# Down projection of nine pairs of feature tiles by seven block products in two passes

## The chip, the core and the metric

The kernel runs on one core of a Trainium2 chip. The core has a matrix engine (TensorE, PE in the profile, with its weight loads as PEld), a vector engine (VectorE, DVE), a scalar engine (ScalarE, ACT), a general engine (GpSimd, POOL) and a queue that issues transfers (SyncE, SP). The metric is the device time of one execution in microseconds; smaller is better.

## The reference

The reference is one decoder layer for 512 tokens of width 1024: a mixer sub-layer (two groups of attention heads), and behind it a SwiGLU channel mixer. Only the end of the channel mixer is touched here:

```python
h = rms_norm(x, ffn_pre_norm)
f = (silu(h @ w_gate) * (h @ w_up)) @ w_down      # 512 x 2816 times 2816 x 1024
x = x + rms_norm(f, ffn_post_norm)
```

D_FF is 2816, which makes 22 feature tiles of 128. All arithmetic is float32.

## The kernel before

**Float32 by three products.** PE multiplies operands of the type fp32r. Each float32 operand is split in two: a high part (ScalarE copies it into an fp32r tile) and a low part (VectorE subtracts the high part from the original). A product of two matrices is then three products in PSUM: high by high, low by high, high by low.

**The gate and up projections.** For feature tiles 3 to 21, `ff_prep` loads the weights of a tile, VectorE and ScalarE form and split block sums, and `ff_seven` multiplies by seven block products instead of eight (a scheme of Winograd's kind) into PSUM tiles called `gw`. VectorE and ScalarE carry the results out (`cy`, `cx`), apply the SiLU and write the feature tile `ffr[f]`: 128 features by 512 tokens, in float32.

**The down projection.** It is what the change replaces. The eight PSUM banks hold the whole output, four token tiles by two column halves (`acc[i][c]`, 128 by 512 each). For each of the 22 feature tiles `down_operands` loads 128 by 1024 weights (tile `wraw`, three buffers), splits them (`whi`, `wlo`) and splits the features (`ffh`, `ffl`); `down` then issues three matmuls of 128x512 for each of the eight banks, so 24 matmuls for a feature tile and 528 in all. For the first 19 feature tiles the loop runs over tiles; the last three (LAST = 3) run with the token tiles outside, so that token tile 0 is finished first and its norm and its output can start while PE works on the next.

**The end.** For each token tile ScalarE squares the two banks and sums them (`junk`), VectorE multiplies by the gain (`uf`), the root is taken in a few small instructions, VectorE scales and adds the residual, and the row goes out.

**What sets the order.** Nothing but the program's own order, and a list scheduler that places the instructions of each engine by its own estimate of times; each engine then executes its queue in that order, waiting on semaphores. `tc.issue_after(before[0])` ties a block product behind the one before it on PE. Tiles come from pools with a fixed number of buffers (`sslot`: 36 slots of 128x512; `big`: eight tiles of 128x1024 and two under the tag `ru`; weights: three each of `raw`, `hi`, `lo`), and an instruction that writes a buffer waits until the last reader of its former contents is done.

In the profile of before, the block products of the gate and up projections are L912, the matmuls of the down projection L1039, the split of weights L104 (ScalarE) and L114 (VectorE), the low part of the features L1033, the square sums L783, the gain L1058, the last scaling L1060, and the output L1061. GpSimd works in the attention part (L517, L672, L651) and in the norms in front of the channel mixer (L807, L819), and on nothing after that.

Of the kernel before, what the change touches and what calls it, by code (L numbers as in the profile page):

```python
# [80 lines left out]
def hybrid_block_kernel(  # L81
# [29 lines left out]
    def split_w(raw, w=1024, lo_eng=None, hi_eng="a"):  # L111
        hi, lo = split_slots()
        to_r(hi_eng, hi[:, :w], raw[:, :w])
        (lo_eng or dve).tensor_tensor(lo[:, :w], raw[:, :w], f32(hi[:, :w]), OP.subtract)  # L114
        return hi, lo
# [912 lines left out]

    def down_operands(f):
        w = split_w(load_w(wd[f]))  # L1030
        hi, lo = sslot("ffh"), sslot("ffl")
        to_r("a", hi, ffr[f])
        dve.tensor_tensor(lo, ffr[f], f32(hi), OP.subtract)  # L1033
        return w, hi, lo

    def down(i, ops, first, last, c):
        w, hi, lo = ops
        for n, (a, wi) in enumerate(((hi, 0), (lo, 0), (hi, 1))):
            pe.matmul(acc[i][c], a[:, i * P:(i + 1) * P],  # L1039
                      w[wi][:, c * SEQ:(c + 1) * SEQ],  # L1040
                      start=(first and n == 0), stop=(last and n == 2))
# [9 lines left out]
    ws = [down_operands(f) for f in range(NF - LAST, NF)]  # L1051
    for i in range(NT):
        for c in range(2):
            for n, ops in enumerate(ws):
# [3 lines left out]
        r = row_rsqrt(a, "c", lambda c: dve.tensor_tensor(uh[c], a[c], g_ffn[:, CS[c]], OP.mult))  # L1058
# [94 lines left out]
```

## Time and profile before

| | us |
|---|---|
| median of three runs | 698.28 (696.29 to 698.91) |
| the profiled execution, device time | 697.03 |
| its span, first to last instruction | 695.3 |
| PE busy in it | 662.0 (95%) |
| DVE busy | 507.7 (73%) |
| ACT busy | 365.3 (53%) |
| POOL busy | 79.0 (11%) |

The device time is 1.73 us more than the span; that part lies around the first and the last instruction. In the views, a row of the timeline or of a group gives start, duration, engine, source line, operation and tiles. Matmuls are pipelined: one of 128x512 is shown with 0.39 us, while the next one starts earlier than that. The column PEclk of the view by windows is the clock that was granted to PE, as a share of the full one.

### The profile page before, as it was taken

What the parts mean: (1) busy time and instruction counts of PE and PEld (TensorE: products, weight loads), DVE (VectorE), ACT (ScalarE), POOL (GpSimd) and SP (SyncE); (2) the same over time, 40 slices, a digit from 0 to 9 for tenths busy, and PEclk for the clock granted to TensorE, in tenths of its full rate; (3) what the DMA queues carried; (4) which work ended last, traced back from release to release, by engine and by line L of the source; (5) the groups of instructions that cost most, each with busy time, mean ns of one, the idle gap of its engine ahead of it and who ended that gap; (6) DMA issues with size and microseconds to landing.
All of it is one profiled execution on the core that took longest, in us unless ns stands there. A gap on an engine that the chain in (4) does not pass through costs nothing.

```text
span 695.3 us, 11168 instructions
## 1 busy us (share of the span) xinstructions
PE 662.0 (95%) x4237; PEld 585.9 (84%) x4237; DVE 507.7 (73%) x918; ACT 365.3 (53%) x775; POOL 79.0 (11%) x86
## 2 busy tenths in 40 slices
PE   8998999999999989998789999999999999999995
PEld 4986878899778877876788999999999998888884
DVE  3867877886999997478898888888888567322227
ACT  6444442556778976435664556555655466211213
POOL 0000000020744632205300000000000000000000
PEclk9999999999999999899899999999999999999998
DMA  8447678571142130165204332333232443233203
GB/s 299 152 137 241 206 256 317 173 255 68 30 130 69 32 107 1 60 203 221 91 32 130 114 121 92 113 102 122 91 111 103 138 135 91 91 99 113 92 1 122
DMA packets 27142, 87.94 MB, mean 126 GB/s; under 512 B 3536, under 2 KB 4432, under 8 KB 26192
## 3 DMA queue, kind: packets, MB, share of 16 engines
q1 hardware_dynamic: 27088, 87.23, 37.4%
q8 instruction: 33, 0.54, 0.3%
q14 instruction: 21, 0.17, 0.1%
HBM read 75.16 MB, written 12.06 MB: 125 GB/s over the span
## 4 chain that ended last, share of the span: by engine, by line
PE 77%; DVE 12%; ACT 4%; DMA 3%; issue 2%; SPq 0%; DVEq 0%; ACTq 0%
PE gw L912 27%; PE acc L1039 17%; PE fm L289 8%; PE gu L892 4%; PE dv L363 3%; PE mixp L683 2%; PE tr L508 2%; DMA wraw<-in_wf 2%; PE avn L636 2%; PE vg L385 2%; PE sc L492 2%; DVE nm L496 2%; PE mix L695 2%; PE sc L493 1%; PE av L559 1%
## 5 line engine op out<-in xcount | busy, mean ns | idle before, releaser
L114 DVE TENSOR_TENSOR wlo<-wraw,whi 128x1024 fp32r<-128x1024 f32 (+2 forms) x58 | 69.9, 1208 | 83.7 <-ACT whi L104 81.1
L104 ACT ACTIVATE whi<-wraw 128x1024 fp32r<-128x1024 f32 (+2 forms) x58 | 60.5, 1046 | 108.5 <-PE acc L1039 66.6
L1039 PE MATMUL acc<-whi,ffl 128*128 128x512 f32 x176 | 68.5, 389 | 0.0
L1039 PE MATMUL acc<-wlo,ffh 128*128 128x512 f32 x176 | 68.0, 389 | 0.0
L1039 PE MATMUL acc<-whi,ffh 128*128 128x512 f32 x176 | 67.1, 390 | 0.4 <-ACT ffh L104 0.4
L517 POOL TENSOR_TENSOR p<-p,l 128x384 f32<-128x384 f32 (+3 forms) x60 | 49.9, 859 | 145.0 <-DVE l L547 88.6
L498 ACT ACTIVATE p<-sc,nm 128x128 f32<-128x128 f32 (+1 forms) x96 | 50.2, 530 | 19.9 <-DVE nm L496 19.5
L496 DVE TENSOR_REDUCE nm<-sc 128x1 f32<-128x128 f32 (+1 forms) x96 | 42.5, 482 | 10.5 <-PE sc L494 7.3
L512 ACT ACTIVATE pth<-tr 128x384 fp32r<-128x384 f32 (+1 forms) x60 | 31.5, 527 | 17.8 <-PE tr L508 17.6
L1039 PEld LDWEIGHTS acc<-whi,ffh 128*128 128x128 f32 x176 | 33.0, 188 | 7.4 <-ACT ffh L104 0.6
L1039 PEld LDWEIGHTS acc<-wlo,ffh 128*128 128x128 f32 x176 | 33.0, 188 | 6.9
L1039 PEld LDWEIGHTS acc<-whi,ffl 128*128 128x128 f32 x176 | 33.0, 188 | 6.8
L289 PE MATMUL fm<-xh,whi 128*128 128x512 f32 x128 | 33.9, 402 | 4.8 <-ACT whi L104 4.8
L513 DVE TENSOR_TENSOR ptl<-tr,pth 128x384 fp32r<-128x384 f32 (+1 forms) x60 | 34.9, 592 | 2.7 <-ACT pth L512 2.5
L492 PE MATMUL sc<-kst,qst 128*128 128x128 f32 (+2 forms) x96 | 35.4, 369 | 1.5 <-DVE pc L593 1.2
L508 PE MATMUL tr<-ident,p 128*128 128x128 f32 x200 | 33.5, 279 | 1.1 <-ACT pct L610 0.7
L289 PE MATMUL fm<-xh,wlo 128*128 128x512 f32 x128 | 33.4, 393 | 0.0
L289 PEld LDWEIGHTS fm<-xh,whi 128*128 128x128 f32 x128 | 23.8, 190 | 11.0 <-ACT whi L104 5.9
L289 PE MATMUL fm<-xl,whi 128*128 128x512 f32 x128 | 32.8, 392 | 0.0
L493 PE MATMUL sc<-kst,qst 128*128 128x128 f32 (+2 forms) x96 | 31.0, 323 | 0.0
L289 PEld LDWEIGHTS fm<-xl,whi 128*128 128x128 f32 x128 | 23.9, 188 | 5.0
L289 PEld LDWEIGHTS fm<-xh,wlo 128*128 128x128 f32 x128 | 23.7, 188 | 4.7
(292 smaller groups left out, 1749.7 us busy)
## 6 DMA issues: line engine op xcount, KB each, us to landing
wraw<-in_wg SPq DMA_DIRECT2D x22, 512.0 KB, 3.4
wraw<-in_wd SPq DMA_DIRECT2D x22, 512.0 KB, 3.4
wu<-in_wu SPq DMA_DIRECT2D x19, 512.0 KB, 3.4
wraw<-in_wf SPq DMA_DIRECT2D x16, 512.0 KB, 4.7
qk<-rope SPq DMA_DIRECT2D x7, 1024.0 KB, 4.8
kst<-qk SPq DMA_DIRECT2D x24, 256.0 KB, 4.2
qst<-qk SPq DMA_DIRECT2D x16, 256.0 KB, 2.8
wraw<-in_wo SPq DMA_DIRECT2D x8, 512.0 KB, 4.3
```

Source lines behind the costliest of these rows:

```text
L104: act.activation(dst, src, AF.Copy)
L114: (lo_eng or dve).tensor_tensor(lo[:, :w], raw[:, :w], f32(hi[:, :w]), OP.subtract)
L289: pe.matmul(pt, w[:, k * P:(k + 1) * P], xx[k], start=(n == 0), stop=(n == 3 * NK - 1))
L492: pe.matmul(sv, lhs, kk[:, 0, :w], start=True, stop=False)
L493: pe.matmul(sv, lhs, kk[:, 1, :w], start=False, stop=False)
L496: dve.tensor_reduce(nm, sv, AX.X, OP.max, negate=True)
L498: act.activation(pt, sv, AF.Exp, bias=nm, accum_out=l[:, i:i + 1])
L508: pe.transpose(tr[:, n * P:(n + 1) * P], pts[i][:, j * P:(j + 1) * P], ident)
L513: dve.tensor_tensor(ptl[:, sl], trv, f32(pth[:, sl]), OP.subtract)
L517: pool.tensor_tensor(p, p, l.to_broadcast(list(p.shape)), OP.mult)
L912: m = pe.matmul(pt, ww[:, k * P:(k + 1) * P], hx[k], start=(start and n == 0), stop=(n == 11), skip_group_check=True)
L1039: pe.matmul(acc[i][c], a[:, i * P:(i + 1) * P], w[wi][:, c * SEQ:(c + 1) * SEQ], start=(first and n == 0), stop=(last and n == 2))
```

## The change

The first 18 feature tiles are taken as nine pairs (PAIRS = 9). For a pair p the product is 512 tokens x 256 features times 256 features x 1024 columns. Each side is cut into 2 x 2 blocks: the tokens into halves (TL, TH), the features into the two tiles (a0, a1), the columns into halves (L, H). The product then takes seven products of blocks, with sums of blocks as operands, instead of eight. A block product is 256 tokens x 128 features x 512 columns, which is 2 token tiles x 3 matmuls = 6 matmuls of 128x512 (`down_mul`). It is done in two passes over the nine pairs, since the partial results don't fit in PSUM at once:

- the x pass: three block products a pair (18 matmuls) into `ca`, `cb`, `cc`. `x_load` fetches 1.5 weight tiles and VectorE subtracts two halves; `x_split` has GpSimd add two quarter blocks of the features (`s1`), and ScalarE and VectorE split weights (`whi`, `wlo`), three quarter blocks of features (`ah`, `al`) and the third weight block (`b21h`, `b21l`).
- the y pass: four block products a pair (24 matmuls) into `cd`, `ca`, `cb`, `cc`. `y_load` fetches the pair's two weight tiles again, and GpSimd subtracts two halves; `y_split` has GpSimd form three sums of feature blocks in place, VectorE two sums of weight blocks, and the two engines split two weight tiles (the second into the tiles `hth`, `htl`, which are free by then) and two feature tiles.

Between the passes ScalarE and VectorE carry `ca`, `cb`, `cc` out of PSUM (`c11`, `p5`); `cc` is then opened anew. After the y pass ten instructions form the four blocks of the output (`part`). The last four feature tiles are done as the last three were before, 24 matmuls each with the token tiles outside, and VectorE adds `part` to the result (`uf`) before the norm, which now reads SBUF (`ug` is the product with the gain).

The scheduler may place the loads and splits of a step ahead of the matmuls of earlier steps; the program itself emits loads four steps ahead (AHEAD) and splits one (AHEADS).

```diff
-LAST = 3
+PAIRS = 9
+LOADS, SPLITS = 3, 2
+AHEAD, AHEADS = 4, 1
...
+    def down_mul(pt, a, b, start, stop):
+        with ExitStack() as es:
+            es.enter_context(tc.issue_after(before[0]))
+            for t in range(2):
+                ts = slice(t * P, (t + 1) * P)
+                for n, (x, y) in enumerate(((a[0], b[0]), (a[1], b[0]), (a[0], b[1]))):
+                    m = pe.matmul(pt[t], x[:, ts], y, start=(start and n == 0), stop=(stop and n == 2),
+                                  skip_group_check=True)
+        before[0] = getattr(m, "ins", m)
+
+    def split_to(hi, lo, src):
+        act.activation(hi, src, AF.Copy)
+        dve.tensor_tensor(lo, src, f32(hi), OP.subtract)
...
+    def x_load(p):
+        r, b21 = raw_tile(p), f32(sslot("b21"))
+        nc.sync.dma_start(r, wd[2 * p])
+        nc.sync.dma_start(b21, wd[2 * p + 1][:, L])
+        dve.tensor_tensor(r[:, H], r[:, L], r[:, H], OP.subtract)
+        xr[p] = r, b21
+
+    def x_split(p):
+        r, b21 = xr.pop(p)
+        a0, a1 = ffr[2 * p], ffr[2 * p + 1]
+        w, b = split_slots(), (sslot("b21h"), sslot("b21l"))
+        split_to(*w, r)
+        ah, al = big("ah", F32R), big("al", F32R)
+        s1 = f32(sslot("s1"))[:, :nhalf]
+        pool.tensor_tensor(s1, a0[:, TH], a1[:, TH], OP.add)
+        for j, (src, sg) in enumerate(((a0[:, TL], 1.0), (a1[:, TL], 1.0), (s1, -1.0))):
+            js = slice(j * nhalf, (j + 1) * nhalf)
+            act.activation(ah[:, js], src, AF.Copy, scale=sg)
+            if sg > 0:
+                dve.tensor_tensor(al[:, js], src, f32(ah[:, js]), OP.subtract)
+            else:
+                dve.scalar_tensor_tensor(al[:, js], src, sg, f32(ah[:, js]), OP.mult, OP.subtract)
+        split_to(*b, b21)
+        xo[p] = [[t[:, j * nhalf:(j + 1) * nhalf] for t in (ah, al)] for j in range(3)], w, b
...
+    def y_load(p):
+        q0 = raw_tile(p)
+        q1 = big("q1")
+        nc.sync.dma_start(q0, wd[2 * p])
+        nc.sync.dma_start(q1, wd[2 * p + 1])
+        pool.tensor_tensor(q0[:, H], q1[:, H], q0[:, H], OP.subtract)
+        yr[p] = q0, q1
+
+    def y_split(p):
+        q0, q1 = yr.pop(p)
+        a0, a1 = ffr[2 * p], ffr[2 * p + 1]
+        pool.tensor_tensor(a0[:, TH], a0[:, TL], a0[:, TH], OP.subtract)
+        pool.tensor_tensor(a0[:, TL], a1[:, TH], a0[:, TH], OP.subtract)
+        pool.tensor_tensor(a1[:, TL], a1[:, TL], a0[:, TL], OP.subtract)
+        dve.tensor_tensor(q0[:, L], q0[:, L], q0[:, H], OP.add)
+        dve.tensor_tensor(q1[:, L], q0[:, L], q1[:, L], OP.subtract)
+        j = 2 * (p % 4)
+        w0, w1 = split_slots(), [t[:, j:j + 2].rearrange("p k t -> p (k t)") for t in (hth, htl)]
+        h0, h1 = ((sslot("ah"), sslot("al")) for _ in range(2))
+        for hl, src in ((w0, q0), (h0, a0), (h1, a1), (w1, q1)):
+            split_to(*hl, src)
+        yo[p] = w0, w1, h0, h1
...
+        mul(cd, h0, TH, w0, H, True)
+        mul(ca, h0, TL, w0, L, False)
+        mul(cb, h1, TL, w1, H, False)
+        mul(cc, h1, TH, w1, L, True)
...
+    for n, (k, p) in enumerate(steps):
+        run("load", load, n + AHEAD + 1)
+        run("split", split, n + AHEADS + 1)
+        mul[k](p)
+        if (k, p) == ("x", PAIRS - 1):
...
+            for t in range(2):
+                dve.tensor_tensor(c11[t], cc[t], c11[t], OP.add)
...
-    for f in range(NF - LAST):
-        ops = down_operands(f)
-        for i in range(NT):
-            for c in range(2):
-                down(i, ops, f == 0, False, c)
...
+            dve.tensor_tensor(uh[c], acc[c], part[i][c], OP.add)
...
+        r = row_rsqrt(uh, "c", lambda c: dve.tensor_tensor(gh[c], uh[c], g_ffn[:, CS[c]], OP.mult))
```

The next two pieces show the queue of VectorE inside the down projection. Before, from the start of the down projection on, it holds the low parts of features (`ffl`, 128x512) and of weights (`wlo`, 128x1024) in this manner:

```order
L1033 TENSOR_TENSOR ffl_6886<-ff6_4686,ffh_6885 128x512
L1033 TENSOR_TENSOR ffl_6920<-ff7_4811,ffh_6919 128x512
L114 TENSOR_TENSOR wlo_6780<-wraw_6777,whi_6779 128x1024
L1033 TENSOR_TENSOR ffl_6954<-ff8_4936,ffh_6953 128x512
L1033 TENSOR_TENSOR ffl_6988<-ff9_5061,ffh_6987 128x512
L1033 TENSOR_TENSOR ffl_7022<-ff10_5186,ffh_7021 128x512
L1033 TENSOR_TENSOR ffl_7056<-ff11_5311,ffh_7055 128x512
L1033 TENSOR_TENSOR ffl_7090<-ff12_5436,ffh_7089 128x512
L114 TENSOR_TENSOR wlo_6814<-wraw_6811,whi_6813 128x1024
```

Now, near the end of the x pass, it holds the following (pair 7 has the feature tiles 14 and 15, pair 8 the tiles 16 and 17; `al` of 128x256 and `wlo_7006` belong to the x pass, `al` of 128x512, `htl` and the `q1` row to the y pass of pairs 0 and 1; the `dr` row, L1094, is the first weight sum of pair 1):

```order
L1069 SCALAR_TENSOR_TENSOR al_6971<-s1_6972,ah_6970 128x256
L1041 TENSOR_TENSOR al_7056<-ff1_3973,ah_7055 128x512
L1094 TENSOR_TENSOR dr_6959<-dr_6959 128x512
L1041 TENSOR_TENSOR htl_3696<-q1_6919,hth_3695 128x1024
L1041 TENSOR_TENSOR al_7102<-ff2_4220,ah_7101 128x512
L1095 TENSOR_TENSOR q1_6960<-dr_6959,q1_6960 128x512
L1041 TENSOR_TENSOR wlo_7006<-dr_6877,whi_7005 128x1024
L1041 TENSOR_TENSOR al_7104<-ff3_4315,ah_7103 128x512
L1067 TENSOR_TENSOR al_7012<-ff16_5936,ah_7011 128x256
L1067 TENSOR_TENSOR al_7012<-ff17_6061,ah_7011 128x256
L1069 SCALAR_TENSOR_TENSOR al_7012<-s1_7013,ah_7011 128x256
```

Where there were two kinds of rows there are seven now. Five instructions of the y pass stand between the last operand of x step 7 and the weights of x step 8, and one more in front of the features of step 8.

GpSimd's queue ended before with the norms in front of the channel mixer:

```order
L672 TENSOR_TENSOR ws_2991<-wraw,ws_2989 128x512
L807 TENSOR_TENSOR u<-mixt,gain 128x512 x4
L819 TENSOR_TENSOR u<-x_0_3687,gain 128x512 x2
L807 TENSOR_TENSOR u<-mixt,gain 128x512 x3
L819 TENSOR_TENSOR u<-x_2_3689,gain 128x512 x2
```

Now 45 instructions follow: nine of L1062 (`s1`), 27 of L1091 to L1093 (the feature sums in place) and nine of L1085 (the weight difference). From the middle of the x pass on they read:

```order
L1062 TENSOR_TENSOR s1_6931<-ff12_5436,ff13_5561 128x256
L1092 TENSOR_TENSOR ff10_5186<-ff11_5311,ff10_5186 128x256
L1091 TENSOR_TENSOR ff12_5436<-ff12_5436 128x256
L1093 TENSOR_TENSOR ff11_5311<-ff11_5311,ff10_5186 128x256
L1062 TENSOR_TENSOR s1_6972<-ff14_5686,ff15_5811 128x256
L1085 TENSOR_TENSOR dr_6918<-q1_6919,dr_6918 128x512
L1091 TENSOR_TENSOR ff14_5686<-ff14_5686 128x256
L1062 TENSOR_TENSOR s1_7013<-ff16_5936,ff17_6061 128x256
```

The sums for the y pass (L1091 to L1093) stand among the sums for the x pass (L1062), pair by pair, and not behind them.

More of the change, by code (lines that the diff above doesn't have):

```diff
@@ L1018, in hybrid_block_kernel @@
         h_split(i, (2, raw4[i]))
+    ncol, nhalf = D_MODEL // 2, SEQ // 2
+    L, H = slice(0, ncol), slice(ncol, D_MODEL)
+    TL, TH = slice(0, nhalf), slice(nhalf, SEQ)
+    xr, xo, yr, yo = {}, {}, {}, {}
+    def down_mul(pt, a, b, start, stop):
[7 more added lines that the diff above has]
+        before[0] = getattr(m, "ins", m)
@@ new lines, in split_to, with raw_tile @@
+    def split_to(hi, lo, src):
+        act.activation(hi, src, AF.Copy)
+        dve.tensor_tensor(lo, src, f32(hi), OP.subtract)
+    def raw_tile(p):
+        if p % 5 in (1, 3):
+            return big("dr", tag="ru")
+        return wpool.tile([P, D_MODEL], F32, tag="raw", name="dr", bufs=WB[0])
+    def x_load(p):
[4 more added lines that the diff above has]
+        xr[p] = r, b21
@@ new lines, in x_mul @@
+    def x_mul(p):
+        (a11, a12, s1), w, b21 = xo.pop(p)
+        first, last = p == 0, p == PAIRS - 1
+        down_mul(ca, a11, [t[:, L] for t in w], first, last)
+        down_mul(cb, s1, [t[:, H] for t in w], first, last)
+        down_mul(cc, a12, b21, first, last)
+    def y_load(p):
[5 more added lines that the diff above has]
+        yr[p] = q0, q1
@@ new lines, in y_mul, with mul @@
+    def y_mul(p):
+        w0, w1, h0, h1 = yo.pop(p)
+        first, last = p == 0, p == PAIRS - 1
+        def mul(pt, h, ts, w, cs, start):
+            down_mul(pt, [t[:, ts] for t in h], [t[:, cs] for t in w], start and first, last)
+        mul(cd, h0, TH, w0, H, True)
+        mul(ca, h0, TL, w0, L, False)
+        mul(cb, h1, TL, w1, H, False)
+        mul(cc, h1, TH, w1, L, True)
+    load, split, mul = {"x": x_load, "y": y_load}, {"x": x_split, "y": y_split}, {"x": x_mul, "y": y_mul}
@@ L1019, in hybrid_block_kernel, with run @@
+    steps = [(k, p) for k in "xy" for p in range(PAIRS)]
+    todo = {"load": list(steps), "split": list(steps)}
+    def run(what, fn, n):
+        while todo[what] and len(steps) - len(todo[what]) < n:
+            k, p = todo[what].pop(0)
+            fn[k](p)
     for f in range(3, NF):
@@ L1022, in hybrid_block_kernel @@
             ff_prep(f + 1)
+        if f == NF - 1:
+            run("load", load, LOADS)
+            run("split", split, SPLITS)
         ff_seven(f)
     late.pop()()
+    ca, cb, cc, cd = (wide(t, "acc") for t in ("tr", "o", "gu", "o"))
+    parts = [f32(rope_tile()) for _ in range(2)]
+    c11, p5, u2, u3 = ([parts[j // 2][:, 2 * (j % 2) + t] for t in range(2)] for j in range(4))
+    for n, (k, p) in enumerate(steps):
[4 more added lines that the diff above has]
+            for t in range(2):
+                act.activation(c11[t], ca[t], AF.Copy)
+            for t in range(2):
+                act.activation(p5[t], cb[t], AF.Copy)
+            for t in range(2):
+                dve.tensor_tensor(c11[t], cc[t], c11[t], OP.add)
@@ L1026, in hybrid_block_kernel @@
+    for t in range(2):
+        act.activation(u2[t], ca[t], AF.Copy)
+    for t in range(2):
+        dve.tensor_tensor(u3[t], cd[t], u2[t], OP.add)
+    for t in range(2):
+        dve.tensor_tensor(u2[t], cb[t], u2[t], OP.add)
+    for t in range(2):
+        dve.tensor_tensor(p5[t], u3[t], p5[t], OP.add)
+    for t in range(2):
+        dve.tensor_tensor(u3[t], u3[t], cc[t], OP.subtract)
+    part = [[c11[0], u2[0]], [c11[1], u2[1]], [u3[0], p5[0]], [u3[1], p5[1]]]
     g_ffn = gain(2)
-    acc = [wide(t, "acc") for t in ("tr", "o", "gu", "o")]
+    LASTF = list(range(2 * PAIRS, NF))
@@ L1029, in down_operands @@
     def down_operands(f):
[L1030 to L1041, printed above, removed]
@@ L1043, in hybrid_block_kernel @@
-    for f in range(NF - LAST):
-        ops = down_operands(f)
-        for i in range(NT):
-            for c in range(2):
-                down(i, ops, f == 0, False, c)
+        raw = load_w(wd[f])
+        w = split_slots() if f < LASTF[0] + 3 else (big("wh", F32R), big("wl", F32R))
+        split_to(*w, raw)
+        hl = sslot("ffh"), sslot("ffl")
+        split_to(*hl, ffr[f])
+        return w, hl
+    ws = [down_operands(f) for f in LASTF]
     for i in range(NT):
```

18 lines of the change are left out of this document (10 added, 8 removed).

## The prediction

> **What bounds the kernel now.** I read the page first, then the chain that ended last from 540 us on, then the windows of the down projection, and last the rows of its tile `acc`.
>
> ```profile
> PE 662.0 (95%) x4237; PEld 585.9 (84%) x4237; DVE 507.7 (73%) x918; ACT 365.3 (53%) x775; POOL 79.0 (11%) x86
> ```
> ```profile
> 567.18 115.93 PE acc L1039 x510
> ```
> ```profile
> core 0: us, PE busy (x) PEld busy (x) DVE busy (x) ACT busy (x) POOL busy (x), PEclk, DMA share, GB/s
> 550.00:560.00 10.00, 10.00 (x87) 10.00 (x86) 3.20 (x5) 3.18 (x7) 0.00 (x0) 1.00 0.63 213
> ...
> 567.20:602.00 34.80, 34.80 (x153) 28.80 (x154) 21.77 (x30) 19.65 (x30) 0.00 (x0) 1.00 0.25 80
> 602.00:687.20 85.20, 85.17 (x376) 70.19 (x374) 24.77 (x39) 19.66 (x33) 0.00 (x0) 1.00 0.24 78
> ```
> ```profile
> L1039 PE MATMUL acc<-whi,ffh x176: 387/389/497, 567.2 to 686.3; 128*128 128x512 f32 x176
> L1039 PE MATMUL acc<-wlo,ffh x176: 388/389/395, 569.1 to 686.8; 128*128 128x512 f32 x176
> ```
>
> The chain is one unbroken run of matmuls from 567.18 on: PE ends last, and nothing else is waited for. The 528 matmuls begin between 567.2 and 686.8, so one begins every 119.6 / 527 = 0.227 us. Beside them VectorE is idle for 60 of the last 85 us and GpSimd does nothing. So a matmul less is worth 0.227 us here, as long as VectorE and GpSimd deliver operands as fast as PE takes them.
>
> **What the change removes.** A pair costs 42 matmuls in place of 48; nine pairs save 54. 54 x 0.227 = 12.3 us off PE's path. That much is certain; what can take it back is the work that makes the block sums.
>
> **What VectorE and GpSimd get.** The prices of VectorE:
>
> ```profile
> L114 DVE TENSOR_TENSOR wlo<-wraw,whi 128x1024 fp32r<-128x1024 f32 x22 | 27.0, 1226 | 63.9 <-ACT whi L104 63.9
> L1033 DVE TENSOR_TENSOR ffl<-ff,ffh 128x512 fp32r<-128x512 f32 x22 | 14.2, 686 | 6.9 <-PE acc L1039 5.8 <-ACT ffh L104 0.9
> L977 DVE TENSOR_TENSOR ff<-cx 128x256 f32<-128x256 f32 x10 | 4.2, 425 | 1.4 <-ACT cx L976 1.2
> ```
> ```profile
> 574.52 1.23 DVE L114 TENSOR_TENSOR wlo<-wraw,whi 128x1024 fp32r<-128x1024 f32 x1 [0.54 <-ACT whi L104]
> 575.66 3.09 DVE L1033 TENSOR_TENSOR ffl<-ff,ffh 128x512 fp32r<-128x512 f32 x5
> ```
>
> Back to back they overlap a little: five of 128x512 take 3.09 us, 0.62 each where one alone lasts 0.69, and the one of 128x1024 is followed after 1.14 us. For 128x256 I take 0.425 - 0.07 = 0.36. An x pair is 0.62 (difference) + 1.14 + 3 x 0.36 + 0.62 = 3.5 us of VectorE beside 18 x 0.227 = 4.1 us of PE; a y pair is 2 x 0.62 + 2 x 1.14 + 2 x 0.62 = 4.8 us beside 24 x 0.227 = 5.4. Alone, VectorE would keep up. But GpSimd is not beside it for nothing:
>
> ```profile
> 315.85 5.05 POOL L807 TENSOR_TENSOR u<-mixt,gain 128x512 f32<-128x512 f32 x4 [17.10 <-DVE mixt L806]
> 322.52 2.98 POOL L819 TENSOR_TENSOR u<-x,gain 128x512 f32<-128x512 f32 x2 [1.62 <-DVE x L810]
> 327.45 1.26 POOL L807 TENSOR_TENSOR u<-mixt,gain 128x512 f32<-128x512 f32 x1 [1.96 <-DVE ss L786]
> ```
> ```profile
> 316.00 1.89 DVE L806 TENSOR_TENSOR mixt<-mix,rope 128x512 f32<-128x512 f32 x3 [0.23 <-PE mix L695]
> ...
> 321.69 1.42 DVE L810 SCALAR_TENSOR_TENSOR x<-u,rs,x 128x512 f32<-128x512 f32 x2
> ...
> 324.30 2.40 DVE L810 SCALAR_TENSOR_TENSOR x<-u,rs,x 128x512 f32<-128x512 f32 x2
> ...
> 327.23 0.15 DVE L786 TENSOR_TENSOR ss<-ss 128x1 f32<-128x1 f32 x1
> 327.41 0.15 DVE L127 TENSOR_SCALAR rr<-ss 128x1 f32<-128x1 f32 x1
> 327.64 1.09 DVE L786 TENSOR_TENSOR ss<-ss 128x1 f32<-128x1 f32 x1
> ```
>
> An addition of one column takes 0.15 us at 327.23 and 1.09 us at 327.64, where it ends at 328.73, 0.02 us behind the GpSimd instruction that ran from 327.45 to 328.71. It waited for GpSimd, though nothing in the program asks for that. L806, which reads one operand from PSUM, ran unhindered beside GpSimd at 316.00. So a VectorE instruction with two operands in SBUF and a GpSimd instruction with two operands in SBUF exclude each other, and all 45 new GpSimd instructions and every VectorE instruction of the two passes, except the sums that read PSUM, are of that kind. What does a turn of GpSimd cost VectorE? The pair at 324.30 takes 2.40 us against 1.42 for the same pair at 321.69: 0.98 us for a GpSimd instruction of which 1.20 us were left (it ended at 322.52 + 2.98 = 325.50). So: its duration less 0.2.
>
> ```profile
> L651 POOL TENSOR_TENSOR ol<-opair,oh 128x512 fp32r<-128x512 f32 x3 | 3.8, 1282 | 1.6 <-ACT oh L104 1.6
> L517 POOL TENSOR_TENSOR p<-p,l 128x512 f32<-128x512 f32 x20 | 21.4, 1069 | 0.0
> L517 POOL TENSOR_TENSOR p<-p,l 128x256 f32<-128x256 f32 x16 | 10.1, 628 | 56.4 <-DVE l L618 31.2 <-PE tr L508 11.2 <-PE av L559 5.2
> ```
>
> L651 is the form of the 512-wide ones: 1.28 - 0.2 = 1.08 us. No row has two full operands of 256; L517, whose second operand is a column, goes from 1069 to 628 ns, a factor of 0.59, so 1.28 x 0.59 = 0.75 and 0.55 as a turn. The bounds are 0.43 (L517's own 0.63 less 0.2) and 0.75 (nothing saved).
>
> The Trainium skill (SBUF — State Buffer, section Who interferes with whom) says that of a VectorE instruction with two SBUF inputs and a GpSimd instruction that reads SBUF the second to issue is fully blocked until the first has finished. The trace agrees that it blocks (1.09 us for 0.15). Read to the letter, a turn would cost its whole duration, 0.75 and 1.28 us, and the sum below would come out 6.2 us higher; the row at 324.30 paid 0.98 of 1.20, and I go by the row.
>
> **The sum for the x pass.** The first pairs are prepared under the last gate and up tiles, where VectorE is busy for 3.2 of 10 us (550 to 560); eleven of the GpSimd instructions fall there and are hidden. PE then enters the x pass at 567.2, as before. VectorE comes out of the gate and up work with its last addition of `cx`:
>
> ```profile
> 565.46 0.69 DVE L967 TENSOR_TENSOR cy<-gw,cy 128x512 f32<-128x512 f32 x1 [1.05 <-PE gw L912]
> ...
> 567.77 0.69 DVE L970 TENSOR_TENSOR cx<-gw,cx 128x512 f32<-128x512 f32 x1
> ```
> ```profile
> wraw<-in_wd SPq DMA_DIRECT2D x22, 512.0 KB, 3.4
> ```
>
> Now between these two stand one subtraction of 512 and five instructions of 256 (2.4 us), a wait of about a microsecond for the load of that subtraction (by my estimate its buffer comes free at 564, and a load lands after 3.4 us), and a GpSimd turn of 0.5: 565.5 + 0.6 + 2.4 + 1.0 + 0.5 = 570.0. From there to the two additions L1145 behind the x pass, which read `cc` out of PSUM, the order has on VectorE 10 instructions of 1024, 30 of 512 (with the `cx` addition and both L1145) and 18 of 256: 11.4 + 18.6 + 6.5 = 36.5 us, y work of the pairs 0 to 4 among it. In the same stretch GpSimd has 25 of 256 and six of 512: 13.8 + 6.5 = 20.2 us. All but the last can't be put off, since the weight sums (L1094) of the pairs 0 to 4 in the same stretch wait for GpSimd's queue up to the fifth L1085. So the second L1145 ends at 570.0 + 36.5 + 20.2 = 626.7.
>
> PE needs it for its matmul number 184: 162 of the x pass and 18 of y step 0 come first, then `mul(cc, ...)` opens `cc` anew. Without waits PE would be there at 567.2 + 183 x 0.227 = 608.7. It comes 18.0 us late, in waits for `wlo` and `al` from x step 5 on, the last and longest in front of `mul(cc, ...)`.
>
> From there on VectorE is ahead: 18 of 1024, 30 of 512 (39.1 us) and three GpSimd turns (3.2 us) stand against 290 matmuls (65.8 us), so the 18 us are neither won back nor added to. ScalarE's high parts (a row each, shorter than VectorE's) and the loads are hidden by the same argument; 17.75 MB in place of 11 is some 140 GB/s in about 125 us, and the window at 550 shows 213.
>
> **The clock.**
>
> ```profile
> 331.78 3.63 PE L830 MATMUL trh<-ident,mixt 128*128 128x128 f32 x16 [4.48 <-ACT mixt L823]
> ```
> ```profile
> 331.80:335.20 3.40, 3.40 (x16) 3.25 (x16) 3.24 (x7) 1.66 (x5) 1.27 (x1) 0.50 0.02 5
> ```
>
> After PE's pause of 4.48 us it was granted half the clock for 3.4 us. In front of `mul(cc, ...)` nine VectorE instructions behind y step 0's weights (about 6 us) and one or two GpSimd turns stand against 14 matmuls (3.2 us), a pause of 4 to 5 us. The stretch at half clock that follows delays the end by 3.4 / 2 = 1.7 us (bounds: none and two of them, 0 to 3.4). Those that fall into the x pass cost nothing, VectorE being later.
>
> The Trainium skill (TensorE: Matmul & The Clock Gate, Part 1) puts the drop to half clock after an idle window of about 3.4 us. The row agrees; by that page the term would be nothing if the pauses stay under 3.4 us, and the sum 703.1.
>
> **The end.**
>
> ```profile
> 688.81 0.15 DVE L786 TENSOR_TENSOR ss<-ss 128x1 f32<-128x1 f32 x1
> 688.88 0.68 DVE L1058 TENSOR_TENSOR uf<-acc,gain 128x512 f32<-128x512 f32 x1
> ```
>
> The last matmul begins at 686.8 and lasts 0.39; `ss` followed 1.6 us behind its end. Now an addition (0.69) and two gain products (2 x 0.62) stand there: 2.0. That is 0.4 us more; the rest of the chain is the same.
>
> **Sum**, on the profiled execution's own 697.03 us: -12.3 + 18.0 + 1.7 + 0.4 = +7.8, so 704.8, said as 705. The median of the runs lies 1.25 above that execution, which is within what I can't resolve.
>
> **The rivals.**
> 1. *The exclusion costs little, and PE stays the bound* (faster). It would do so if GpSimd's turns fell into pauses of VectorE: alone VectorE needs 36.5 us where PE needs 41.5 up to matmul 184, and it waits for weight buffers when ahead. The point that decides is x step 5: if its `wlo` is in time there, no lag builds up. Against it: GpSimd's 20 us are four times those pauses. 697.03 - 12.3 + 0.4 = 685.1.
> 2. *The exclusion is cheaper by half* (no change). With 0.43 a turn, VectorE's own instructions shortened by 0.07 each when they have waited (31 x 0.07 = 2.2) and no clock term: 18.0 - 3.0 - 2.2 = 12.8, and 697.03 - 12.3 + 12.8 + 0.4 = 697.9.
> 3. *The exclusion is dearer, with loads behind it* (slower still). Turns at full duration add 6.2; a GpSimd difference (L1085) that waits for its two loads, 3.4 us each behind SP's other waits, holds the sums queued behind it and VectorE behind these. 711 and more.
>
> **How the numbers follow.** Forecast (about 700 to 709) 0.55, rival 1 0.13, rival 2 0.20, rival 3 0.12. Half a per cent, 3.5 us, is about what a measurement of this kernel can tell from no change. Faster by more: rival 1, and 0.02 of rival 2's low side: 0.15. Within it: the rest of rival 2 and the low edge of the forecast, 0.20. Slower: 0.65. The range 695 to 712 leaves out rival 1 and a part of rival 3. The cases that are slower have 700 to 712 for their own.
>
> **What would show it.** Right: `al` and `wlo` of the x pass as PE's releasers, from step 5 on; VectorE busy without a gap from 570 to 627; rows of GpSimd at 128x256 near 0.75 and longer where VectorE is in front; VectorE rows of 128x256 with a mean well over 0.425; L1145 ending some 18 us later than 608; then PE without waits to the end. Wrong: PE busy throughout the x pass (rival 1), waits on `q1` or `dr` loads (rival 3), or waits in the y pass, of which the sum has none.

## The result, and the profile after

| | before | after |
|---|---|---|
| median of four runs each, us | 698.13 (696.29 to 698.91) | 706.76 (704.23 to 708.70) |
| ratio to before, 95% interval | 1 | 1.0125 (1.0082 to 1.0169) |
| profiled execution, device time / span, us | 697.03 / 695.3 | 704.23 / 702.5 |

The change saves 54 of 4237 matmuls and the kernel is slower by 1.25%. 705.0 was forecast, with a range of 695 to 712. The page's busy times:

```profile
PE 660.2 (94%) x4183; PEld 579.0 (82%) x4183; DVE 584.6 (83%) x1008; ACT 390.4 (56%) x826; POOL 131.2 (19%) x131
```

VectorE has 90 instructions more than before and 77 us more of busy time; GpSimd has the 45 sums, 52 us. The windows of the down projection (columns as before: length, PE, PEld, DVE, ACT, POOL, each with its instructions, then granted clock, DMA share, GB/s):

```profile
567.20:602.00 34.80, 30.62 (x123) 23.71 (x121) 33.31 (x36) 18.80 (x36) 28.59 (x25) 0.95 0.49 161
602.00:630.00 28.00, 21.27 (x68) 15.00 (x69) 28.00 (x33) 17.44 (x27) 11.53 (x9) 0.82 0.63 212
630.00:660.00 30.00, 30.00 (x131) 24.27 (x130) 28.68 (x34) 15.69 (x19) 4.32 (x2) 1.00 0.31 101
```

From 569.2 to 630 it is VectorE that has no gap, and PE that pauses. In front of that VectorE waited once, 1.4 us, for a load:

```profile
569.21 0.69 DVE L1052 TENSOR_TENSOR dr<-dr 128x512 f32<-128x512 f32 x1 [1.40 <-DMA dr<-in_wd]
```

From 630 on PE is busy throughout again. The chain that ended last says the same, piece by piece: up to 626.6 it consists of VectorE's instructions and of the issue times between them, then of matmuls alone.

```profile
593.57 1.21 DVE wlo L1041
594.79 1.21 DVE al L1067 x2
596.00 0.88 DVE al L1069
596.88 1.15 DVE dr L1094
598.02 1.15 DVE b21l L1041
...
624.72 1.24 DVE al L1041
625.97 0.61 DVE rope L1145
626.62 46.07 PE acc L1035 x195
672.69 19.35 PE acc L1181 x84
```

L1145 is the addition that frees `cc`; its second instance ends at 626.6. What PE waited for between 566 and 630, from the view of the waits:

```profile
PE acc L1035 <- DVE al L1067: 5.1, 2, 2.8
PE acc L1035 <- ACT rope L1143: 3.1, 2, 2.4
PE acc L1035 <- DVE cx L972: 2.4, 1, 2.4
PE acc L1035 <- DVE wlo L1041: 0.3, 1, 0.3
```

VectorE's low parts, ScalarE's copies of `cb` between the passes (L1143), and the last addition of `cx`; PE itself waited for no load. The first and the last group of the stage's matmuls:

```profile
L1035 PE MATMUL acc<-whi,ah x72: 389/396/628, 566.1 to 669.0; 128*128 128x512 f32 x72
...
L1181 PE MATMUL acc<-wl,ffh x8: 392/397/397, 678.2 to 694.4; 128*128 128x512 f32 x8
```

The 474 matmuls begin between 566.1 and 694.4, 128.3 us, where the 528 of before took 119.6. Measured against one matmul each 0.227 us from the first on, matmul 16 begins 2.6 us late, number 128 8.1, number 148 12.4, number 175 15.7, number 185 19.4, number 201 19.8 and the last one 20.9. So the balance inside the stage is -12.3 + 20.9 = +8.6. The stage began 1.1 us earlier than before, and 8.1 us lie behind the start of the last matmul in place of 8.5: +7.2 in the span.

**How VectorE lost the time.** The timeline from 595.7 on, first VectorE, then GpSimd (start, duration, line, tiles):

```profile
595.92 0.96 DVE L1069 SCALAR_TENSOR_TENSOR al<-s,ah 128x256 fp32r<-128x256 f32 x1
596.80 1.23 DVE L1094 TENSOR_TENSOR dr<-dr 128x512 f32<-128x512 f32 x1
597.95 1.23 DVE L1041 TENSOR_TENSOR b21l<-b,b21h 128x512 fp32r<-128x512 f32 x1
599.10 1.78 DVE L1095 TENSOR_TENSOR q<-dr,q 128x512 f32<-128x512 f32 x1
```
```profile
595.74 0.85 POOL L1092 TENSOR_TENSOR ff<-ff,ff 128x256 f32<-128x256 f32 x1 [0.36 <-DVE al L1067]
596.56 0.92 POOL L1091 TENSOR_TENSOR ff<-ff 128x256 f32<-128x256 f32 x1
597.43 1.19 POOL L1093 TENSOR_TENSOR ff<-ff,ff 128x256 f32<-128x256 f32 x1
598.58 1.75 POOL L1085 TENSOR_TENSOR dr<-q,dr 128x512 f32<-128x512 f32 x1
```

The two engines take turns. GpSimd ends at 596.59, 597.48, 598.62 and 600.33; VectorE ends each time some 0.3 to 0.6 us behind it. Two instructions of 128x512 follow each other after 1.15 us (596.80, 597.95, 599.10) instead of 0.62, so a GpSimd instruction of 128x256 costs 0.53; the one that stands beside L1085 lasts 1.78, 1.09 more than the 0.69 of one alone. The prediction had 0.55 and 1.08. Over the stretch from 567 to 640 VectorE's groups read:

```profile
L1041 DVE TENSOR_TENSOR wlo<-dr,whi 128x1024 fp32r<-128x1024 f32 x11 | 16.5, 1504 | 0.0
L1041 DVE TENSOR_TENSOR al<-ff,ah 128x512 fp32r<-128x512 f32 x15 | 16.1, 1080 | 0.0
L1041 DVE TENSOR_TENSOR b21l<-b,b21h 128x512 fp32r<-128x512 f32 x7 | 9.0, 1281 | 0.1
...
L1145 DVE TENSOR_TENSOR rope<-acc,rope 128x512 f32<-128x512 f32 x2 | 1.4, 678 | 0.0
```

1504 ns where one alone lasts 1226, and 1080 and 1281 for 686. L1145, with one operand in PSUM, stays at 678.

### The profile page after: what moved, and what is told of

Its sections match the earlier page's. It is cut to its first block, busy times and chain, and to the rows that moved or that the text cites. A ratio compares the mean times of both kernels' runs of the same rounds, so it can differ in the third digit from the quotient of the medians.

```text
span 702.5 us, 11371 instructions
## 1 busy us (share of the span) xinstructions
PE 660.2 (94%) x4183; PEld 579.0 (82%) x4183; DVE 584.6 (83%) x1008; ACT 390.4 (56%) x826; POOL 131.2 (19%) x131
## 5 line engine op out<-in xcount | busy, mean ns | idle before, releaser
L106 ACT ACTIVATE whi<-wraw 128x1024 fp32r<-128x1024 f32 (+2 forms) x36 | 37.1, 1037 | 41.3 <-PE fm L291 14.1
L116 DVE TENSOR_TENSOR wlo<-wraw,whi 128x1024 fp32r<-128x1024 f32 (+2 forms) x36 | 43.0, 1198 | 20.5 <-ACT whi L106 20.4
L1062 POOL TENSOR_TENSOR s<-ff,ff 128x256 f32<-128x256 f32 x9 | 8.6, 959 | 214.7 <-DVE ff L979 209.4
L1035 PE MATMUL acc<-whi,al 128*128 128x512 f32 x72 | 29.6, 411 | 5.1 <-DVE al L1067 5.1
L291 PEld LDWEIGHTS fm<-xh,whi 128*128 128x128 f32 x128 | 24.1, 193 | 10.7 <-ACT whi L106 5.3
L1035 PE MATMUL acc<-wlo,ah 128*128 128x512 f32 x72 | 29.6, 414 | 0.3 <-DVE wlo L1041 0.3
L1035 PE MATMUL acc<-whi,ah 128*128 128x512 f32 x72 | 29.4, 411 | 0.0
L510 PEld LDWEIGHTS tr<-ident,p 128*128 128x128 f32 x200 | 23.5, 144 | 4.2 <-DVE ptl L515 1.5
L1041 DVE TENSOR_TENSOR wlo<-dr,whi 128x1024 fp32r<-128x1024 f32 x18 | 25.0, 1391 | 0.0
```

Source lines behind the costliest of these rows:

```text
L106: act.activation(dst, src, AF.Copy)
L291: pe.matmul(pt, w[:, k * P:(k + 1) * P], xx[k], start=(n == 0), stop=(n == 3 * NK - 1))
L510: pe.transpose(tr[:, n * P:(n + 1) * P], pts[i][:, j * P:(j + 1) * P], ident)
L1035: m = pe.matmul(pt[t], x[:, ts], y, start=(start and n == 0), stop=(stop and n == 2), skip_group_check=True)
L1041: dve.tensor_tensor(lo, src, f32(hi), OP.subtract)
```

## The experiments

Theory A is the prediction's: GpSimd's sums exclude VectorE's instructions, and so their time adds to VectorE's in the x pass. Its rivals: B, VectorE or PE waits for GpSimd's results or for buffers that GpSimd holds; C, VectorE alone is too slow; D, the order in VectorE's queue alone is at fault. All edits are made to the changed kernel, or to another one where that is said. Kernels with sums left out are read for their time alone. The ratios are to runs of before beside each kernel, whose medians went from 697.18 to 698.13 us, and the change's own times from 704.23 to 708.70. So a difference of two medians below can be off by a few us where the change is one of the two, and by one or two elsewhere.

| kernel | us, median | ratio to before, 95% interval |
|---|---|---|
| the change | 706.76 | 1.0125 (1.0082 to 1.0169) |
| no sums | 686.83 | 0.9854 (0.9840 to 0.9869) |
| unread sums of the weights and features | 705.22 | 1.0122 (1.0093 to 1.0151) |
| fills in place of sums | 686.97 | 0.9858 (0.9832 to 0.9885) |
| fills three times | 688.75 | 0.9870 (0.9849 to 0.9890) |
| unread sums of features alone | 702.35 | 1.0062 (1.0037 to 1.0086) |
| all sums on VectorE | 693.66 | 0.9951 (0.9929 to 0.9973) |
| feature sums on VectorE | 697.21 | 0.9996 (0.9979 to 1.0012) |
| weight differences on VectorE | 702.07 | 1.0064 (1.0044 to 1.0083) |
| strict order | 698.60 | 1.0011 (0.9994 to 1.0028) |
| strict order, all sums on VectorE | 694.94 | 0.9967 (0.9953 to 0.9981) |
| the same, differences and `cc` additions later | 694.85 | 0.9963 (0.9948 to 0.9978) |
| the same, `s1` on GpSimd | 694.73 | 0.9965 (0.9951 to 0.9978) |

### Without the sums

```
-        pool.tensor_tensor(s1, a0[:, TH], a1[:, TH], OP.add)
+        s1 = a0[:, TH]
...
-        pool.tensor_tensor(q0[:, H], q1[:, H], q0[:, H], OP.subtract)
...
-        pool.tensor_tensor(a0[:, TH], a0[:, TL], a0[:, TH], OP.subtract)
-        pool.tensor_tensor(a0[:, TL], a1[:, TH], a0[:, TH], OP.subtract)
-        pool.tensor_tensor(a1[:, TL], a1[:, TL], a0[:, TL], OP.subtract)
```

> The changed kernel without the 45 instructions of GpSimd in the down projection: the operands are then the unsummed blocks, which leaves these sums out of the output. VectorE's and ScalarE's work and the matmuls stay as they are. Theory A (a VectorE instruction and a GpSimd instruction with two operands in SBUF each exclude each other, so that the 20.2 us of GpSimd's turns add to VectorE's own work in the x pass): without turns VectorE needs 38.7 us from its last addition of cx to the second L1145 in this kernel's order, from about 569.5, so 608.2 against PE's 608.7; no lag, 685 us (684 to 689). Theory B (VectorE merely waits for GpSimd's results, since GpSimd is slow and its queue is held up by loads): the same 685, so this run does not tell A from B. Theory C (VectorE alone is too slow here, its instructions being longer than alone because ScalarE, PE and the loads use SBUF too, and y work standing ahead in its queue): 700 or more, with the same waits for wlo and al.

686.83 us. The last matmul is 2.9 us late in place of 20.9. C falls: the same VectorE work, y work ahead of x work included, is done in time when GpSimd is silent. The sums cost 706.76 - 686.83 = 19.9 us as GpSimd makes them (18.9 by the ratios of the two).

### Sums that nobody reads, of weights and features

```
-        pool.tensor_tensor(q0[:, H], q1[:, H], q0[:, H], OP.subtract)
+        pool.tensor_tensor(scr, q1[:, H], q0[:, H], OP.subtract)
```

(and the feature sums in the same manner; `scr` is read by nobody)

> As the kernel without sums, but GpSimd executes 45 additions and subtractions of the same shapes on the same operands, and writes the result to a spare tile that nobody reads. No VectorE, ScalarE or PE instruction waits for a value from GpSimd; the sums are left out of the output as there. Theory A: the turns are back, so the lag is back: VectorE 36.9 us and GpSimd about 20 us in the x pass, 700 to 707 us, near 704. Theory B: nothing waits for GpSimd, so 685 (684 to 689). Theory C: 700 or more, here as without sums.

705.22 us, the number that A gave, but not in A's way. PE was on time up to matmul 175 and then waited 9.0 us at once for ScalarE's copy of `cb` (L1144 here). VectorE itself had gaps:

```profile
DVE dr L1095 <- DMA dr<-in_wd: 6.2, 1, 6.2
DVE al L1042 <- ACT ah L1041: 2.1, 1, 2.1
```

In this kernel's order the weight differences stand ahead in GpSimd's queue, and since they read the weight tiles, these buffers came free only after GpSimd. One of the differences (L1086) is shown with 16.48 us from 592.22 on, while VectorE went on without a gap up to 607.5; a load of `q1` waited 7.5 us for it, and the load of `dr` on which VectorE then waited 6.2 us was issued behind that one. The run mixes the exclusion with held buffers and decides nothing between A and B. A later run repeats it without the weights.

### Fills in place of sums

```
-        pool.tensor_tensor(s1, a0[:, TH], a1[:, TH], OP.add)
+        pool.memset(s1, 0.5)
```

(for each of the five kinds)

> The changed kernel with each of the 45 sums replaced by GpSimd filling the same destination with a constant: every wait for GpSimd's results stays, but GpSimd reads nothing (the sums are left out of the output). Theory A as I hold it (the exclusion is of instructions that both read two operands from SBUF): no turns, VectorE 39.4 us from 569.5, so 608.9 against PE's 608.7: 685 to 690 us. Theory B: the waits stay; by how much depends on how long a fill lasts, between 685 (if fills are far shorter than 0.75 us) and 704. If instead any GpSimd instruction excludes VectorE, reading or not: the mean of VectorE's 128x256 differences stays above 0.5 us and the time follows the length of the fills.

686.97 us. A fill of 128x256 lasted 0.31 us and one of 128x512 0.53. Every instruction that waited for a sum waits for its fill, and VectorE's difference of 128x256 lasted 420 ns, where one alone lasts 425. Since fills are short, B could still hold; hence the next.

### Fills as long as the sums

```
-        pool.tensor_tensor(s1, a0[:, TH], a1[:, TH], OP.add)
+        for _ in range(3):
+            pool.memset(s1, 0.5)
```

> As the run in which GpSimd only fills the sums' destinations, but each fill is done three times, so that GpSimd is busy for 0.94 us in place of each sum of 256 and for 1.58 in place of each of 512 (about 48 us, as the 52 of the changed kernel), and every wait for GpSimd's results stays. The sums are left out of the output. Theory A (two-operand reads exclude each other): no turns, VectorE's rows stay at 0.42, 0.69 and 1.22 us, 686 to 690 us. Theory B (GpSimd's results come too late, since GpSimd is slow and works in order): the lag comes back, 698 to 706.

688.75 us. The page of this kernel, and VectorE's groups from 567 to 640:

```profile
PE 653.6 (95%) x4183; PEld 576.2 (84%) x4183; DVE 558.6 (81%) x1008; ACT 390.5 (57%) x826; POOL 123.0 (18%) x221
```
```profile
L1041 DVE TENSOR_TENSOR wlo<-dr,whi 128x1024 fp32r<-128x1024 f32 x15 | 18.2, 1216 | 1.7 <-ACT whi L1040 1.7
L1041 DVE TENSOR_TENSOR al<-ff,ah 128x512 fp32r<-128x512 f32 x18 | 12.0, 681 | 0.0
...
L1099 DVE TENSOR_TENSOR dr<-dr 128x512 f32<-128x512 f32 x9 | 6.1, 683 | 2.2 <-POOL dr L1087 2.2
...
L1041 DVE TENSOR_TENSOR b21l<-b,b21h 128x512 fp32r<-128x512 f32 x7 | 4.8, 683 | 0.1
```

GpSimd is busy for 123.0 us against 131.2 in the changed kernel, with the same instructions waiting for it, and VectorE waits for it 2.2 us in all. VectorE's queue is in a slightly different order, with three rows more up to the second addition that frees `cc`, and is done with that at 612.0 all the same. Its rows are those of VectorE alone: 1216, 681, 683 ns. That GpSimd is busy or in front costs 1.9 us (688.75 - 686.83); the other 18 are there when GpSimd reads its operands. B falls as the main cause.

### Unread sums that hold nothing back

```
+        pool.tensor_tensor(spare[:, TL], f32(ah[:, :nhalf]), a0[:, TH], OP.add)
+        pool.tensor_tensor(spare, a0, a1, OP.add)
+        for ts in (TL, TH):
+            pool.tensor_tensor(spare[:, TL], a0[:, ts], a1[:, ts], OP.add)
         split_to(*b, b21)
```

(in `x_split` of the kernel without sums; `spare` is read by nobody)

> The kernel without sums (the sums are left out of the output), with VectorE's queue unchanged, and GpSimd in each x step adding feature tiles into a spare tile that nobody reads: three additions of 128x256, the first of which waits for the step's ah, and one of 128x512. Unlike in the run with the unread sums, GpSimd reads no weight tile, so it holds no weight buffer and no load back. Theory A (exclusion): five or six of the nine steps lie behind VectorE's last addition of cx, 5.5 x (3 x 0.55 + 1.08) = 15 us of turns on top of VectorE's 38.7: 569.5 + 38.7 + 15 = 623 against PE's 608.7, a lag of 14.5, 1.7 of half clock: 701 us (697 to 704), with VectorE's rows of 128x256 and 128x512 longer by the turns. Theory B (only waits for GpSimd's results or for buffers that it holds cost time): 687 us, as without sums.

702.35 us: 15.5 more than without sums, with VectorE's queue unchanged row by row and nobody waiting for a result. One load of `q1` did wait for a buffer that GpSimd read (6.7 us), but VectorE had no gap from 566.5 to 653, so that did not matter there. VectorE's groups from 567 to 640:

```profile
L1042 DVE TENSOR_TENSOR wlo<-dr,whi 128x1024 fp32r<-128x1024 f32 x13 | 18.4, 1424 | 0.0
...
L1067 DVE TENSOR_TENSOR al<-ff,ah 128x256 fp32r<-128x256 f32 x14 | 9.5, 720 | 0.0
L1042 DVE TENSOR_TENSOR b21l<-b,b21h 128x512 fp32r<-128x512 f32 x7 | 7.4, 1070 | 0.0
```

720 in place of 420 ns, 1070 in place of 686. Together with the long fills this shows the exclusion: reading alone brings the loss, and being busy and waited for alone does not. All these sums read two operands; whether one would do was not tried.

The forecast of 701 came out, but not by turns at an even price. Up to 597 GpSimd's 20 sums behind 567 were let in, most of them beside a VectorE row that was longer for it. The next one was not:

```profile
602.51 19.40 POOL L1070 TENSOR_TENSOR junkb<-ah,ff 128x256 bf16<-128x256 f32 x1 [5.89 <-DVE dr L1094]
```

While it stood there, VectorE went through more than 20 rows back to back at their undisturbed length. It ended at 621.91, beside the first addition that frees `cc`, which reads one operand from PSUM. So the exclusion holds GpSimd off as well, and by this row for much longer than one VectorE instruction; the 16.48 us in the run with unread sums of weights and features is the same picture. (GpSimd's spans are rough in these profiles, but VectorE's undisturbed rows are not.) What lets GpSimd in the one time and not the other was not tried.

The Trainium skill (SBUF — State Buffer, section Who interferes with whom) says that a VectorE instruction with two SBUF inputs contends with a GpSimd instruction that reads SBUF, not with one that only writes it. These two runs agree: 415 ns beside fills, 720 beside sums. The same page (Summary: rules for kernel authors) has the second of the two blocked until the first has finished. There the measurement differs: VectorE paid 0.53 us for a sum whose shortest rows in the changed kernel last 0.73 to 0.79, and the 19.40 us are many VectorE instructions and not one.

### The same sums on VectorE

```
-        pool.tensor_tensor(s1, a0[:, TH], a1[:, TH], OP.add)
+        dve.tensor_tensor(s1, a0[:, TH], a1[:, TH], OP.add)
```

(for all five kinds)

> The changed kernel with all 45 sums on VectorE instead of GpSimd; nothing is left out. Theory A: VectorE pays 0.36 us for a sum of 256 and 0.62 for one of 512 in place of turns of 0.55 and 1.08. Its order has 46.9 us from the last addition of cx to the second L1145, from about 569.5, so 616.4 against 608.7: a lag of 7.7, and 1 or 2 us of half clock: 693 us (690 to 697), so 10 to 14 less than the change, though VectorE has more to do. Theory B: VectorE no longer waits for another engine but carries the sums itself; 690 to 697 as well. Theory C: VectorE is the bound and gets 10 us more: 712 or more.

693.66 us (693 expected), 13.1 less than the change, though VectorE has 45 instructions more. Matmul 201 is 8.6 us late (7.7 expected). It has the lowest median of the kernels here that compute everything, 0.49% below before, with an interval of 0.27 to 0.71%; the intervals of three kernels further down overlap with it.

### One half of the sums each

The first half:

```
-        pool.tensor_tensor(s1, a0[:, TH], a1[:, TH], OP.add)
+        dve.tensor_tensor(s1, a0[:, TH], a1[:, TH], OP.add)
...
-        pool.tensor_tensor(a0[:, TH], a0[:, TL], a0[:, TH], OP.subtract)
+        dve.tensor_tensor(a0[:, TH], a0[:, TL], a0[:, TH], OP.subtract)
```

(and the two sums behind it)

> The changed kernel with the 36 feature sums on VectorE and only the nine weight differences (128x512) on GpSimd; nothing is left out. Theory A: 43.8 us of VectorE's own from 569.5 to the second L1145, and five or six turns of 1.08 in that stretch: 569.5 + 43.8 + 6 = 619.3 against 608.7, a lag of 10.6, and 1.7 of half clock: 697 us (694 to 700). Theory B (waits for GpSimd's results): only the weight differences can be waited for then, 690 or less.

697.21 us (697 expected). The weight differences that are left on GpSimd did not cost turns throughout: VectorE waited for them three times, 3.6 us in all.

The second half:

```
-        pool.tensor_tensor(q0[:, H], q1[:, H], q0[:, H], OP.subtract)
+        dve.tensor_tensor(q0[:, H], q1[:, H], q0[:, H], OP.subtract)
```

> The other half: the nine weight differences on VectorE, the 36 feature sums on GpSimd; nothing is left out. Theory A: 40.1 us of VectorE's own, and 25 turns of 0.55: 569.5 + 40.1 + 13.8 = 623.4 against 608.7, a lag of 14.7, and 1.7 of half clock: 701 us (698 to 704). If a turn of a feature sum costs no more than VectorE's own sum (0.36), it would be 697 as the other half.

702.07 us (701 expected). The feature sums give back 9.6 us when VectorE makes them, the weight differences 4.7; together 14.3, beside the 13.1 of both at once. With 36 and nine instructions, a sum of 256 by GpSimd would be 0.27 us dearer than by VectorE on the mean, hidden ones included, and one of 512 0.52. Both rest on the change's median, whose interval is about 3 us to either side, so only the order of size is shown.

### The order of the y work

```
             k, p = todo[what].pop(0)
+            if what == "load":
+                fn[k](p)
+                continue
+            tied[:], made[:] = made, []
+            with ExitStack() as es:
+                for m in tied:
+                    es.enter_context(tc.issue_after(getattr(m, "ins", m)))
+                fn[k](p)
```

(`made` collects a step's splits and sums on VectorE and GpSimd)

> The changed kernel with each step's splits and sums tied behind those of the step before on VectorE and on GpSimd, so that no y work stands ahead of x work; nothing is left out. Theory A: the x pass has no lag then (VectorE 28.7 us to the second L1145), but VectorE's and GpSimd's work of the y pass still has to be done one after the other. Up to the last y step that is 569.5 + 28.7 + 35.6 + 26.2 = 660 against the 647.6 at which PE without waits would begin it: the lag of some 12 us comes in the y pass, and the time is 698 us (694 to 702), 8 less than the change. Rival D (the cost is the order alone: y work ahead of x work in VectorE's queue): 685 to 689, PE without waits.

698.60 us (698 expected). PE is 1.0 us late at the end of the x pass, 8.6 at matmul 201 and 13.7 at number 251. In the y pass it waits for weights, and for the addition (L1154) and the copies (L1152) between the passes:

```profile
PE acc L1036 <- DVE wlo L1042: 3.7, 3, 2.6
PE acc L1036 <- DVE rope L1154: 2.0, 1, 2.0
PE acc L1036 <- ACT rope L1152: 1.6, 1, 1.6
```

D holds a part of the loss: 8 of the 20 us. Without the y work in front, the x pass is free, and the lag moves to the y pass, where 12 us remain. That the turns still have to be taken explains a part of these; the next run shows how much.

The same edit, with all sums on VectorE:

```
-        made.append(pool.tensor_tensor(s1, a0[:, TH], a1[:, TH], OP.add))
+        made.append(dve.tensor_tensor(s1, a0[:, TH], a1[:, TH], OP.add))
```

(for all five kinds)

> The same order, and all 45 sums on VectorE; nothing is left out. Theory A: VectorE alone has 34.3 us to the second L1145 and 47.9 more up to the last y step: 569.5 + 34.3 + 47.9 = 651.7 against 647.6, a lag of 4: 689 us (687 to 693), less than the 693.7 of the sums on VectorE in the scheduler's order. Rival D: the 10 us more of VectorE's own make no difference to the strict order with GpSimd; both at 685 to 689.

694.94 us: the forecast of 689 was wrong by 6. Only 3.7 of the 12 us went with GpSimd, though VectorE now makes the sums itself. In the x pass VectorE was not busy throughout (29.8 of 35 us between 567 and 602). The group of L1086, from 567 to 650:

```profile
L1086 DVE TENSOR_TENSOR dr<-q,dr 128x512 f32<-128x512 f32 x9 | 6.2, 689 | 4.6 <-DMA q<-in_wd 3.2 <-DMA dr<-in_wd 1.3
```

The weight differences stood in VectorE's queue and waited there for their loads. The next run takes them out of the way.

```
     def y_load(p):
...
-        dve.tensor_tensor(q0[:, H], q1[:, H], q0[:, H], OP.subtract)
...
     def y_split(p):
         q0, q1 = yr.pop(p)
         a0, a1 = ffr[2 * p], ffr[2 * p + 1]
+        made.append(dve.tensor_tensor(q0[:, H], q1[:, H], q0[:, H], OP.subtract))
...
+            run("split", split, n + AHEADS + 2)
+            with tc.issue_after(getattr(made[-1], "ins", made[-1])):
-            for t in range(2):
-                dve.tensor_tensor(c11[t], cc[t], c11[t], OP.add)
+                for t in range(2):
+                    dve.tensor_tensor(c11[t], cc[t], c11[t], OP.add)
```

> The strict order with all sums on VectorE, and two more edits: the weight difference of a y step stands with the step's split instead of with its loads, and the two additions that read cc stand behind y step 1's weights. In the strict order VectorE waited 4.6 us for loads at these differences. Nothing is left out. Theory A: 36.3 us to the second addition, 45.8 more up to the last y step: 569.5 + 36.3 + 45.8 = 651.6 against 647.6, and no waits of VectorE: a lag of 4, 689 us (687 to 692). If it is not the waits that cost the strict order its 5 us, it stays at 695.

694.85 us, the same as before the edit. VectorE does not wait for those loads any more, but for other things (567 to 660):

```profile
DVE al L1068 <- PE acc L1036: 3.4, 1, 3.4
DVE wlo L1042 <- ACT whi L1041: 2.9, 4, 1.0
DVE dr L1053 <- DMA dr<-in_wd: 1.0, 1, 1.0
```

It is busy for 28.0 of the 35 us from 567 to 602, less than before the edit. The first row shows why: `al` needs a buffer that PE has not finished with. In strict order VectorE runs ahead of PE only as far as the buffers reach, and then stands still; what it could have done in that time is missing in the y pass, where the last y step comes 10.7 us late. The sum had taken VectorE as never idle. That the buffers bound it was not tried by another run, for instance with more of them.

To this kernel one more edit:

```
-        made.append(dve.tensor_tensor(s1, a0[:, TH], a1[:, TH], OP.add))
+        made.append(pool.tensor_tensor(s1, a0[:, TH], a1[:, TH], OP.add))
```

> As the run before, with the nine sums s1 of the x pass back on GpSimd, which does most of them before the x pass, while VectorE still has pauses; the 36 other sums stay on VectorE. Theory A: 2.5 us less of VectorE's own work in the x pass against two to four turns of 0.55: about 1 us less than the run before, 688 us. If every GpSimd instruction costs a whole turn: 1 us more, 690.

694.73 us, no difference to the run before that could be told. VectorE was waiting for buffers in that pass, so neither outcome of the expectation could show.

## Why the prediction was right

- **The matmuls, -12.3.** Held in number. Their pace did not hold quite: without any long wait, in the kernel with fills, the first matmul of the x pass begins at 569.4 and its last one, number 162, at 607.0:

```profile
L1035 PE MATMUL acc<-whi,ah x72: 387/395/402, 569.4 to 654.4; 128*128 128x512 f32 x72
...
L1035 PE MATMUL acc<-b21l,ah x18: 392/396/397, 572.7 to 607.0; 128*128 128x512 f32 x18
```

  That is 37.6 / 161 = 0.233 us each in place of 0.227, 1.0 us over the pass and some 2 over the stage. The prediction had no such term. It is why the kernel without sums comes to 686.8 and not to the first rival's 685.1.
- **The price of a turn, 0.55 and 1.08.** Measured 0.53 and 1.09 in the timeline.
- **The sum for the x pass, 570.0 to 626.7.** The second L1145 ended at 626.6, and VectorE had no gap behind 569.2. That the end fits to 0.1 us is partly luck: the last addition of `cx` came at 571.4 and not at 570.0, and from there it took 55.2 us in place of 56.7. Matmul 184 was 19.0 us late in place of 18.0; PE had entered the stage 1.1 us earlier in this execution. In kind the sum is right for its reason: GpSimd without reads gives 687 to 689, reads without results 702.
- **Where the waits begin.** The step said from x step 5 on, with PE entering the x pass undisturbed. In truth PE waited 2.4 us at matmul 16 already, for `cx` (L972), which stood on VectorE behind the wait of 1.4 us for a load and a turn of GpSimd. That cost nothing of its own, since VectorE was later still at matmul 184. The waits for `al` came at matmuls 128 and 147, in x steps 7 and 8 and not from step 5 on. And the last and longest wait was to stand in front of `mul(cc, ...)`: the longest was 2.8 us for `al`, and in front of `mul(cb, ...)` PE waited 3.1 us for ScalarE's copies of `cb`, of which the sum had nothing. With these and the half clock PE was itself nearly as late as VectorE when it came to matmul 184 (matmul 183 began at 625.9), so a faster L1145 alone would have gained little.
- **The clock, 1.7.** Mis-sized. The half clock came mostly up to the second L1145, before which matmul 184 could not begin anyhow:

```profile
620.00:626.60 6.60, 4.57 (x9) 2.55 (x9) 6.60 (x11) 6.00 (x9) 2.17 (x2) 0.59 0.80 289
626.60:630.00 3.40, 3.38 (x12) 2.79 (x13) 3.40 (x4) 1.70 (x2) 0.50 (x1) 0.80 0.25 48
```

  Behind it 0.4 us were lost up to matmul 201, and 1.1 more up to the last matmul by the slower pace. The two make 1.5, and so the total came out by luck; the term did not. The other reading, no half clock with pauses under 3.4 us, did not hold either: PE's longest pause was 2.8 us (and not 4 to 5), and the granted clock was 0.59 in the first of these windows.
- **The end, +0.4.** Measured -0.4 from the last matmul's start to the end of the span. `ss` began 2.3 us after that start in place of 2.0, and what follows `ss` was shorter by 0.7; the sum had left it the same.
- **The y pass without waits** held: the lateness grows from 19.8 to 20.9 over 273 matmuls, without a step.
- **The rivals.** The first needed GpSimd's turns to cost little, and they cost 18 us. The second put a turn at 0.43, which is a fifth less than 0.55 and not the half that its name says; measured was 0.53. The third had loads behind L1085: GpSimd did wait for loads there,

```profile
L1085 POOL TENSOR_TENSOR dr<-q,dr 128x512 f32<-128x512 f32 x9 | 16.6, 1845 | 17.5 <-DMA dr<-in_wd 9.4 <-DMA q<-in_wd 5.4 <-DVE dr L1094 2.4
```

  but VectorE had other work in that time and no gap behind 569.2, so these loads did not hold it up.

## What to carry to other kernels

Before work goes to GpSimd to relieve VectorE, look whether both read two operands from SBUF at the same time: here 45 sums cost some 20 us on GpSimd and 7 on VectorE itself. In such a stage add the two engines' times as one, up to the point where PE needs the result. And a sum that takes an engine as never idle needs the buffers that let it run ahead: the forecasts of the strict order with the sums on VectorE took it so and missed by 6 us; that the buffers are the reason was argued and not tried.

## What was new about the hardware

- GpSimd's fills (0.31 us for 128x256, 0.53 for 128x512) left VectorE's two-operand instructions at their undisturbed length, even with GpSimd busy for 24 of 35 us.
- When both queues were full, the engines alternated one by one for long stretches of the changed kernel, and GpSimd paid as well: its sums of 128x256 had means of 0.90 to 1.15 us, and those of 128x512 1.85.
- In other kernels a GpSimd sum that became ready while VectorE ran without a pause stood for 19.40 us (128x256, unread sums of features) and 16.48 us (128x512, unread sums of both), with VectorE's rows at their undisturbed length beside it.
- Matmuls of the same form, with no wait and the clock granted in full, began 0.233 us apart in the x pass and 0.227 in the kernel before. What makes the difference was not tried.
